# Two layers of a hybrid diffusion backbone on one core: stores taken off SP's queue, and the second layer's modulation vectors made in the first layer's out-projection

## The chip, the cores and the metric

The kernel runs on 1 core of one Trainium2 chip. The metric is the device time of one execution in microseconds. The median of 3 runs of the kernel before is 5156.44 us (5150.59 to 5167.15).

## What is computed

Two layers (DEPTH 2) work on 512 latent tokens and 256 context tokens of width 1024. In the kernel the 768 tokens are six tiles of 128 rows: tiles 0 and 1 are context, 2 to 5 latent. Each layer of the reference, cut to what matters here:

```python
sh_a, sc_a, g_a, sh_f, sc_f, g_f = jnp.split((silu(c) @ w_mod[l] + b_mod[l])[:, None, :], 6, axis=-1)
csh_a, csc_a, cg_a, csh_f, csc_f, cg_f = jnp.split(silu(c_ctx) @ w_mod[l] + b_mod[l], 6, axis=-1)
y_c, y_l = _hybrid_mixer(_modulate(s_ctx, csh_a, csc_a), _modulate(x, sh_a, sc_a), ang, need_ctx,
                         w_in[l], w_out[l], ml, rw, mla)       # mLSTM, RWKV-7, attention; concat @ w_out
x = _ln_affine(ALPHA * x + g_a * y_l, ln_mix_g[l], ln_mix_b[l])
h_l = _modulate(x, sh_f, sc_f)                                 # the context likewise, in the first layer
y = _peer(h, peer_w_q[l], peer_keys[l], peer_u[l], peer_v[l])  # 8 heads, top 16 of 16384 experts
x = _ln_affine(ALPHA * x + g_f * y_l, ln_ffn_g[l], ln_ffn_b[l])
```

The vectors sh, sc and g of a layer depend only on c and c_ctx and on that layer's w_mod (1024 x 6144, 25.2 MB): they can be made at any time before their layer begins.

## The kernel before, in words

**The stages of a layer**, one after the other: modulated input and input projection; attention (`mla`) woven with the mLSTM's projection; the mLSTM woven with RWKV's projection (`mlstm`, `project_rwkv`); `rwkv`; the out-projection (`project_out`) with the residual and LayerNorm of each tile; the PEER ranking (`scores`); then routing and gates, with expert blocks computed early (`early`, 38 of 128 blocks in the first layer, 34 in the second) beside gathers of single experts; the dense stage over all expert blocks (`dense`: A = u·h, gelu and gates, acc += v·c); and the last residual (`final` for gathered tiles, the loop below it for dense ones). In the first layer the dense tiles are the latents 2 to 5 and the gathered ones the context's 0 and 1; in the second 2, 3, 4 and 5.

**Order.** `weave` interleaves generators by the numbers beside them, and a scheduler then fixes one list of instructions for each engine. An engine, and a queue of DMAs that an engine issues, goes through its list in order: an instruction whose inputs or buffers aren't ready holds up what stands behind it. Nearly all loads and stores are issued by SP (`nc.sync`); POOL (`nc.gpsimd`) issues gathers of expert rows (L1601) and a few stores; ACT issues none.

**Modulation** (`modulation`, L320 on). A round r makes 2048 columns: per step k four tiles of 128 x 512 of w_mod (256 KB each, tag "wmod") are loaded (L333) and multiplied with silu(c) into one PSUM bank (L338; g runs 3, 2, 1, 0), eight steps to a round, then bias, transposes, and four stores of the rows to DRAM (L347). The first round of layer 0 stands in the setup. The other two of layer 0 and all three of layer 1 are woven into layer 0's mLSTM stage, with 8 buffers:

```python
gens.append((chain(self.modulation(w, 0, (1, 2), 1, 8), self.modulation(w, 1, (0, 1, 2), 1, 8)), 51))
```

**The out-projection** (L1199 on) loads eight slabs of w_out (tag "wout", 3 buffers), splits each on ACT and DVE into a high and a low part (wo0hi, wo0lo, ...), and for each of the tiles 3, 4, 2, 5, 0, 1 loads the concatenated mixer output (ycat), transposes it and runs 48 matmuls (L1239). The caller runs it to the tenth yield in layer 0, then emits the latents' hidden transposes (`hidden`, L1289), then the rest.

**Early blocks** load ut (L1259), split it (L1266 ACT, L1267 DVE or POOL), run 24 matmuls (L1497), gelu on ACT (tile c, L1499), and store c to DRAM (L1512). Gates are built on PE and ACT in a tile "stage" and stored in four pieces (L1484, 112 of them). Both stores stand on SP's queue between the loads of ut.

**Dense and last residual.** Before the dense stage the residual inputs of the dense tiles (xn, L368), one of the gathered (xr), and a gate row are loaded on SP. Layer 1's modulated input finds the latents kept in SBUF, and loads the context (xt) from DRAM again.

## Time and profile before

| | |
|---|---|
| median of 3 runs | 5156.44 us (5150.59 to 5167.15) |
| the profiled execution's own time | 5153.65 us |
| its span | 5151.7 us |
| mean granted TensorE clock | 0.941 |
| busy: PE, weight loads, DVE, ACT, POOL | 89%, 75%, 71%, 36%, 40% |
| DMA | 991.60 MB, mean 192 GB/s |

The page of the profile has the span in 40 slices: PE is full (9 tenths or more) in two long stretches, the dense stages of the two layers, and at 6 to 9 tenths elsewhere. All times below are microseconds from the start of the span. Layer 0's stages lie about so: mLSTM stage 377 to 628, rwkv to 965, out-projection to 1091 with the start of the ranking, routing and early blocks 1240 to 1645, dense to 2850; layer 1: mLSTM 3222 to 3404, out-projection from 3713, routing and early blocks 3920 to 4189, dense 4199 to 5104. A group of instructions reads "busy, mean ns of one, idle before it and what ended the idle time". In the chain of waits each line is a piece of time and what the end of the span was waiting for in it. A duration of a DMA in the chain runs from its issue to its landing; on a queue ("SPq") it is the time that the queue's issuing took, waits between the issues of one row included.

### The profile page before, as it was taken

How to read it: one execution, taken by the hardware profiler on the slowest of the kernel's cores; microseconds unless marked ns; L12 is line 12 of the kernel's file. 1: busy time of each engine (PE TensorE's matmuls, PEld its weight loads, DVE VectorE, ACT ScalarE, POOL GpSimd, SP SyncE). 2: the span in 40 equal slices, each digit the busy share in tenths (PEclk: the TensorE clock that was granted, in tenths of full speed). 3: DMA queues.
4: the chain of work that ended last, by engine and by line, in shares of the span. 5: the costliest groups of instructions: out<-in, count | busy, mean ns of one | idle time of the engine just before them, and what ended most of it. 6: DMA issues, size and time to landing. Idle time of an engine off the chain costs nothing.

```text
span 5151.7 us, 89696 instructions
## 1 busy us (share of the span) xinstructions
PE 4604.4 (89%) x35473; PEld 3857.8 (75%) x35473; DVE 3676.4 (71%) x7469; ACT 1848.1 (36%) x3330; POOL 2065.0 (40%) x1761
## 2 busy tenths in 40 slices
PE   6998888888987999999999689978778889999998
PEld 4675567667876887778878467767667888988887
DVE  4444455679885999999999734545579757777777
ACT  2342255232553222222222223345433543333332
POOL 1102333244773555555555210233336634444442
PEclk9998889999998999999999898989989999999999
DMA  4016400321477999999999310100222578999994
GB/s 144 22 43 220 159 4 5 122 83 56 170 284 255 352 342 329 347 342 343 346 335 339 104 34 23 45 22 3 85 96 91 214 269 311 320 316 316 315 319 173
DMA packets 402933, 991.60 MB, mean 192 GB/s; under 512 B 35104, under 2 KB 167584, under 8 KB 401744
## 3 DMA queue, kind: packets, MB, share of 16 engines
q1 hardware_dynamic: 289552, 574.91, 32.2%
q0 software_dynamic: 112960, 410.96, 22.1%
q8 instruction: 279, 4.57, 0.4%
q14 instruction: 142, 1.16, 0.1%
HBM read 894.45 MB, written 91.19 MB: 191 GB/s over the span
## 4 chain that ended last, share of the span: by engine, by line
PE 64%; DVE 15%; POOL 6%; DMA 5%; issue 5%; ACT 4%; SPq 1%; POOLq 0%; DVEq 0%; ACTq 0%
PE acc L1564 17%; PE A L1497 15%; PE b L446 6%; PE b L1355 4%; PE spill L1564 3%; PE b L1497 2%; PE b L1239 2%; DMA c<-early 1%; PE b L799 1%; PE b L1479 1%; PE b L826 1%; PE b L530 1%; DVE py L1617 1%; POOL eq L1430 1%; DMA ut<-in_u_t 1%
## 5 line engine op out<-in xcount | busy, mean ns | idle before, releaser
L1601 POOL DMA_INDIRECT rows<-in_u,eid x384 | 538.3, 1402 | 565.6 <-DVE act L1613 251.8
L1601 POOL DMA_INDIRECT rows<-in_v,eid x384 | 517.0, 1346 | 559.2 <-DVE py L1617 324.4
L1564 PE MATMUL acc<-vhi,clo 128*128 128x512 f32 x1536 | 600.8, 391 | 0.0
L1564 PE MATMUL acc<-vt,chi 128*128 128x512 f32 x1536 | 600.5, 391 | 0.0
L1564 PE MATMUL acc<-vhi,chi 128*128 128x512 f32 x1536 | 599.1, 390 | 0.0
L1497 PE MATMUL A<-hh,uhi 128*128 128x384 f32 (+1 forms) x1472 | 541.1, 368 | 25.5 <-ACT uhi L1266 22.7
L1497 PE MATMUL A<-hh,ut 128*128 128x384 f32 (+1 forms) x1472 | 540.1, 367 | 12.5 <-DVE ut L1267 12.5
L1497 PE MATMUL A<-hl,uhi 128*128 128x384 f32 (+1 forms) x1472 | 540.4, 367 | 0.0
L1266 ACT ACTIVATE uhi<-ut 128x1024 fp32r<-128x1024 f32 x256 | 271.1, 1059 | 629.7 <-PE A L1497 521.7
L1617 DVE SCALAR_TENSOR_TENSOR py<-rows,act,py 128x1024 f32<-128x1024 f32 x381 | 492.4, 1292 | 1.9
L1613 DVE CUSTOM_DVE_ANT_0 rows<-rows,hrow 128x1024 f32<-128x1024 f32 x384 | 463.7, 1240 | 12.2 <-DMA rows<-in_u,eid 12.2
L1266 ACT ACTIVATE vhi<-vt 128x1024 fp32r<-128x1024 f32 x256 | 270.8, 1058 | 555.0 <-PE spill L1564 334.6
L446 PE MATMUL b<-hT,winhi 128*128 128x512 f32 (+1 forms) x1360 | 382.3, 372 | 6.7 <-ACT winhi L1266 4.8
L1267 DVE TENSOR_TENSOR ut<-ut,uhi 128x1024 fp32r<-128x1024 f32 x212 | 275.5, 1299 | 119.6 <-ACT uhi L1266 77.7
L1564 PEld LDWEIGHTS acc<-vhi,clo 128*128 128x128 f32 x1536 | 288.8, 188 | 61.2 <-DVE clo L1253 0.3
L1564 PEld LDWEIGHTS acc<-vhi,chi 128*128 128x128 f32 x1536 | 289.0, 188 | 59.0 <-ACT chi L1252 0.3
L1564 PEld LDWEIGHTS acc<-vt,chi 128*128 128x128 f32 x1536 | 289.0, 188 | 58.9
L1497 PEld LDWEIGHTS A<-hh,uhi 128*128 128x128 f32 x1472 | 278.3, 189 | 62.9 <-ACT uhi L1266 23.5
L1497 PEld LDWEIGHTS A<-hh,ut 128*128 128x128 f32 x1472 | 278.6, 189 | 47.1 <-DVE ut L1267 14.1
L1267 DVE TENSOR_TENSOR vt<-vt,vhi 128x1024 fp32r<-128x1024 f32 x256 | 312.2, 1220 | 1.5 <-PE spill L1564 0.6
L1497 PEld LDWEIGHTS A<-hl,uhi 128*128 128x128 f32 x1472 | 278.5, 189 | 36.1
L446 PEld LDWEIGHTS b<-hT,winhi 128*128 128x128 f32 x1360 | 245.9, 204 | 64.7 <-issue 26.1
(544 smaller groups left out, 10560.7 us busy)
## 6 DMA issues: line engine op xcount, KB each, us to landing
ut<-in_u_t SPq DMA_DIRECT2D x256, 512.0 KB
vt<-in_v SPq DMA_DIRECT2D x256, 512.0 KB
gates<-stage SPq DMA_DIRECT2D x112, 512.0 KB
wmod<-in_w_mod SPq DMA_DIRECT2D x160, 256.0 KB
gt<-gates SPq DMA_DIRECT2D x32, 1024.0 KB
win<-in_w_in SPq DMA_DIRECT2D x52, 512.0 KB
gt<-gates SPq DMA_DIRECT2D x32, 768.0 KB
wq<-in_w_q SPq DMA_DIRECT2D x32, 512.0 KB
```

The costliest lines, as they stand in the source:

```text
L446: self.nc.tensor.matmul(ps[:, :n], lhsT=w[u][:, k, :], rhs=self.hT[v][:, k, c:c + n], start=k + u + v == 0, stop=k == KT - 1 and u == 1)
L530: nc.tensor.matmul(pss[t // 2 * 2][:, t % 2 * 256:t % 2 * 256 + 256], lhsT=self.hT[u][:, j * 4 + k, t * 128:(t + 1) * 128], rhs=wi[v][:, k ...
L799: nc.tensor.matmul(ps[:, :w], lhsT=qTs[h][:, t * 128:(t + 1) * 128], rhs=self.kT[:, h, c0:c0 + w], start=True, stop=True)
L1239: nc.tensor.matmul(ps, lhsT=yT[u][:, k, :], rhs=ws[k][v][:, cs], start=k + u + v == 0, stop=k == KT - 1 and u == 1)
L1266: self.nc.scalar.activation(out=hi, in_=x, func=AF.Copy)
L1267: lo_eng.tensor_tensor(out=lo, in0=x, in1=hi.bitcast(F32), op=ALU.subtract)
L1355: nc.tensor.matmul(ps[:, :n], lhsT=(wh, wl)[x][:, k, :], rhs=(hi, lo)[y][:, k, :], start=k + x + y == 0, stop=k == KT - 1 and x == 1)
L1497: nc.tensor.matmul(bank[:, :n], lhsT=us[x][:, k, :], rhs=(hi, lo)[y][:, k, :], start=k + x + y == 0, stop=k == KT - 1 and x == 1)
L1564: nc.tensor.matmul(b, lhsT=cs[x][:, t * 128:(t + 1) * 128], rhs=vs[y][:, h * 512:(h + 1) * 512], start=s0 and x + y == 0, stop=s1 and x == 1)
L1601: nc.gpsimd.indirect_dma_start(out=r, out_offset=None, in_=a[tab], in_offset=bass.IndirectOffsetOnAxis(ap=eid[:, i:i + 1], axis=0))
L1613: nc.vector.tensor_tensor_reduce(out=r, in0=r, in1=h, scale=1.0, scalar=0.0, op0=ALU.mult, op1=ALU.add, accum_out=act[:, i:i + 1])
L1617: nc.vector.scalar_tensor_tensor(out=y, in0=r, scalar=act[:, i:i + 1], in1=y, op0=ALU.mult, op1=ALU.add)
```

## The change

1. **Stores off SP.** The stores of modulation rows (L347), of mLSTM output y (L738), of the mixer residual (L1194, L1651) and the loads of ycat (L1207), and around the last residual the gate row, xn, xr and the vectors, are issued by POOL. The stores of gi and gf (L471, L472), of the attention output (L829), of the gates (L1484) and of the early blocks (L1512) are issued by ACT.
2. **Layer 1's modulation** leaves the mLSTM stage (its number in the weave goes from 51 to 21) and is emitted in layer 0's out-projection, three yields after each of the ten yields of it, with 7 buffers for "wmod".
3. **Room for that:** two buffers for "wout" (3 before), one gate tile for both streams, 6 buffers for gathered rows (`ROWS`, 7 before).
4. **The context's residual tiles stay in SBUF** beside the latents' (xs for all six tiles), so that layer 1 loads no xt; layer 0 loads no xr, and its last residual runs on DVE alone.

```diff
-ROWS = 7
+ROWS = 6
 def modulation(...)
-                nc.sync.dma_start(out=dr[:, r, g], in_=rows[32 * g:32 * g + 2, :])
+                nc.gpsimd.dma_start(out=dr[:, r, g], in_=rows[32 * g:32 * g + 2, :])
...
-            nc.sync.dma_start(out=o[n][0:4, :], in_=msc[r:r + 4, :])
+            nc.scalar.dma_start(out=o[n][0:4, :], in_=msc[r:r + 4, :])
...
-                nc.sync.dma_start(out=self.y[t * 128:(t + 1) * 128, 0:256], in_=yL[:, t, :])
+                nc.gpsimd.dma_start(out=self.y[t * 128:(t + 1) * 128, 0:256], in_=yL[:, t, :])
...
-                nc.sync.dma_start(out=self.y[t * 128:(t + 1) * 128, 640:1024], in_=yM[:, t, :])
+                nc.scalar.dma_start(out=self.y[t * 128:(t + 1) * 128, 640:1024], in_=yM[:, t, :])
...
-                            gens.append((chain(self.modulation(w, 0, (1, 2), 1, 8), self.modulation(w, 1, (0, 1, 2), 1, 8)), 51))
+                            gens.append((self.modulation(w, 0, (1, 2), 1, 8), 21))
...
 def residual(...)
-                (q or nc.sync).dma_start(out=d, in_=x)
+                nc.gpsimd.dma_start(out=d, in_=x)
...
 def project_out(...)
-            nc.sync.dma_start(out=y, in_=self.y[t * 128:(t + 1) * 128, :])
+            nc.gpsimd.dma_start(out=y, in_=self.y[t * 128:(t + 1) * 128, :])
...
-            w = self.t(pw, [128, D], "wout", 3)
+            w = self.t(pw, [128, D], "wout", 2)
...
-            gate = self.gate_rows(p, l, 2, s, f"gate{s}")
+            gate = self.gate_rows(p, l, 2, s, "gate")
...
-                    nc.sync.dma_start(out=G[tk // 32, :, i:i + 32, :], in_=st[:, i:i + 32, :])
+                    nc.scalar.dma_start(out=G[tk // 32, :, i:i + 32, :], in_=st[:, i:i + 32, :])
...
-            self.nc.sync.dma_start(out=done[i], in_=c)
+            self.nc.scalar.dma_start(out=done[i], in_=c)
...
                 out = self.project_out(w, v, l, need, x, hold)
+
+                late = self.modulation(w, 1, (0, 1, 2), 1, 7) if need else iter(())
                 for _ in range(10 if need else 8):
                     next(out)
+                    for _ in range(3):
+                        next(late, None)
                 spans = [self.hidden(pe, w, l, 1, dn if need else dn + ga, [] if need else ga)]
                 hi, lo = (z[:, :, :T * 128] for z in spans[0])
+                self.all(late)
                 self.all(out)
...
-                        nc.sync.dma_start(out=d, in_=x)
+                        nc.gpsimd.dma_start(out=d, in_=x)
...
-                gate = self.gate_rows(ln, l, 5, 1, "gate1")
+                gate = self.gate_rows(ln, l, 5, 1, "gate1", q=nc.gpsimd)
                 xn = self.keep.enter_context(pool("xn", "right")) if need else ln
-                xs = {t: self.load_x(xn, t, f"xn{t}", 1) for t in dn}
+                xs = {t: self.load_x(xn, t, f"xn{t}", 1, nc.gpsimd) for t in dn + (ga if need else [])}
...
-                    xr = {ga[0]: self.load_x(ln, ga[0], "xr", 1)}
...
-                        x = xr[t] if t in xr else self.load_x(ln, t, "xr", 1)
+                        x = xs[t] if need else self.load_x(ln, t, "xr", 1, nc.gpsimd)
...
-                        self.residual(w, l, "f", tiles, [xs[t] for t in tiles], zs, rows, nc.vector if tiles[-1] == TURN[T][-1] else nc.gpsimd, None, FQ and nc.gpsimd, FM and nc.gpsimd)
+                        self.residual(w, l, "f", tiles, [xs[t] for t in tiles], zs, rows, nc.vector if need or tiles[-1] == TURN[T][-1] else nc.gpsimd, None, FM and nc.gpsimd)
```

Where instructions move, the lists of the engines show it. First SP's list where layer 0's out-projection begins, before (gate rows, slabs of w_out, residual inputs xk):

```order
L1207 DMA ycat_10941<-y_149 128x1024
L361 DMA gate_2085_11347<-mod_rows_69 128x1024
L1214 DMA wout_10885<-in_w_out 128x1024
L1214 DMA wout_10891<-in_w_out 128x1024
L1214 DMA wout_10897<-in_w_out 128x1024
L368 DMA xk_2021_10939<-in_x 128x1024
L1214 DMA wout_10903<-in_w_out 128x1024
L1214 DMA wout_10909<-in_w_out 128x1024
L1214 DMA wout_10915<-in_w_out 128x1024
```

and the same place of the changed kernel, where the tiles of w_mod stand among the slabs (96 of them before the keys and w_q of the ranking are loaded):

```order
L332 DMA wmod_10685<-in_w_mod 128x512
L332 DMA wmod_10687<-in_w_mod 128x512
L1212 DMA wout_10541<-in_w_out 128x1024
L1212 DMA wout_10547<-in_w_out 128x1024
L367 DMA xk_1916_10597<-in_x 128x1024
L332 DMA wmod_10689<-in_w_mod 128x512
L367 DMA xk_1958_10774<-in_x 128x1024
L1212 DMA wout_10553<-in_w_out 128x1024
L1212 DMA wout_10559<-in_w_out 128x1024
L332 DMA wmod_10691<-in_w_mod 128x512
```

The seven tiles wmod_10673 to wmod_10689 fill the seven buffers; wmod_10691 is the eighth, and takes the buffer of wmod_10673. On PE of the changed kernel the second step of the modulation stands among the matmuls of the out-projection so:

```order
L1238 MATMUL b_10618<-wo3hi_10561,yT_1918_10601 128x512
L1238 MATMUL b_10644<-wo2hi_10555,yT_1919_10602 128x512
L1238 MATMUL b_10644<-wo3hi_10561,yT_1918_10601 128x512
L337 MATMUL b_10670<-wmod_10691,cvec_75 32x512
L337 MATMUL b_10670<-wmod_10689,cvec_75 32x512
L337 MATMUL b_10670<-wmod_10687,cvec_75 32x512
L337 MATMUL b_10670<-wmod_10685,cvec_75 32x512
L1238 MATMUL b_10795<-wo0hi_10543,yT_1961_10779 128x512
```

Each step begins with the tile that was loaded last, and the step before it ended with wmod_10673. All 24 steps stand ahead of the latents' hidden transposes, the last four of them with nothing between. Then SP's list where layer 0 goes from the early blocks to the dense stage, before:

```order
L1512 DMA early_119_16956<-c_16954 128x512
L1512 DMA early_122_16994<-c_16992 128x512
L1512 DMA early_126_17026<-c_17024 128x512
L368 DMA xn_3167_17045<-x_m_11243 128x1024
L368 DMA xn_3168_17047<-x_m_11039 128x1024
L368 DMA xn_3169_17049<-x_m_11141 128x1024
L368 DMA xn_3170_17051<-x_m_11345 128x1024
L1259 DMA ut_17071<-in_u_t 128x1024
L1259 DMA vt_17073<-in_v 128x1024
L1536 DMA gt_17075<-gates_10870 128x16x128
```

and changed:

```order
L1258 DMA ut_16882<-in_u_t 128x1024
L1258 DMA ut_16923<-in_u_t 128x1024
L1258 DMA ut_16961<-in_u_t 128x1024
L1258 DMA ut_17073<-in_u_t 128x1024
L1258 DMA vt_17075<-in_v 128x1024
L1535 DMA gt_17077<-gates_10528 128x16x128
L1258 DMA vt_17079<-in_v 128x1024
```

The stores of the last early blocks and the loads of xn no longer stand ahead of the dense stage's first ut (ut_17073 here, ut_17071 before).

## Rows read from the trace of the kernel before

**Rows 1.** The page, part 1: busy time, share of the span, instructions.

```profile
PE 4604.4 (89%) x35473; PEld 3857.8 (75%) x35473; DVE 3676.4 (71%) x7469; ACT 1848.1 (36%) x3330; POOL 2065.0 (40%) x1761
```

**Rows 2.** Windows: length, PE PEld DVE ACT POOL busy, granted clock, DMA share, GB/s.

```profile
377.00:628.00 251.00, 221.83 (x1479) 151.35 (x1477) 109.05 (x319) 60.56 (x138) 69.67 (x95) 0.90 0.61 199
...
1240.00:1645.00 405.00, 340.68 (x1949) 298.51 (x1948) 325.42 (x499) 194.09 (x393) 265.02 (x185) 0.92 0.60 218
...
2260.00:2290.00 30.00, 27.64 (x120) 21.92 (x119) 27.26 (x35) 8.16 (x11) 14.26 (x12) 1.00 1.04 396
...
3222.00:3404.00 182.00, 161.02 (x1079) 134.69 (x1077) 92.59 (x232) 58.93 (x131) 59.73 (x81) 0.92 0.12 35
...
3920.00:4189.00 269.00, 232.34 (x1525) 228.67 (x1523) 196.59 (x275) 144.64 (x293) 171.40 (x115) 0.92 0.53 193
```

**Rows 3.** Waits of SP's queue: total us, times, longest.

```profile
SPq L1207 <- DMA y<-yR: 586.1, 2, 306.8
...
SPq L1512 <- ACT c L1499: 266.5, 59, 16.8
```

**Rows 4.** Groups of instructions, PE, 376 to 640: busy, mean ns, idle before.

```profile
L338 PE MATMUL b<-wmod,cvec 128*32 128x512 f32 x320 | 46.1, 650 | 7.6 <-DMA wmod<-in_w_mod 7.5
```

**Rows 5.** Chain of waits, 376 to 640: shares, then start and us.

```profile
by line: PE b L446 32.0%; PE b L338 11.7%; DMA wmod<-in_w_mod 8.3%; PE b L686 4.3%; PE b L653 3.9%; POOL mv L557 3.1%; issue 2.8%; POOL mixed_r L557 2.0%; PE b L672 1.8%; PE b L569 1.7%; PE b L679 1.5%; PE b L701 1.3%; PE b L661 1.2%; POOL 
...
387.63 2.80 DMA wmod<-in_w_mod
...
408.04 4.96 DMA wmod<-in_w_mod
```

**Rows 6.** Timeline of PE, 395 to 425: start, us, what.

```profile
398.09 1.07 PE L338 MATMUL b<-wmod,cvec 128*32 128x512 f32 x8
...
405.63 1.06 PE L338 MATMUL b<-wmod,cvec 128*32 128x512 f32 x8
```

**Rows 7.** Timeline of PE, layer 0's out-projection.

```profile
965.25 0.79 PE L1239 MATMUL b<-wo0lo,yT 128*128 128x512 f32 x1 [1.53 <-DVE wo0lo L1253]
...
1027.70 2.04 PE L1289 MATMUL b<-consts_g,xk 128*128 128x128 f32 x16
```

**Rows 8.** Timeline of SP's queue, layer 1's out-projection.

```profile
3718.44 2.60 SPq L1214 DMA_DIRECT2D wout<-in_w_out  x3
...
3725.26 2.06 SPq L1214 DMA_DIRECT2D wout<-in_w_out  x2
```

**Rows 9.** Timeline of SP's queue, layer 0, from early blocks to dense.

```profile
1609.68 16.20 SPq L1512 DMA_DIRECT2D early<-c  x3
...
1629.95 6.55 SPq L1259 DMA_DIRECT2D vt<-in_v  x1
...
1637.03 0.43 SPq L1259 DMA_DIRECT2D ut<-in_u_t  x1
```

**Rows 10.** Groups of instructions, PE, 1595 to 1665.

```profile
L1497 PE MATMUL A<-hh,uhi 128*128 128x512 f32 x17 | 7.9, 466 | 13.1 <-ACT uhi L1266 11.7 <-ACT c L1499 1.4
...
L1497 PE MATMUL A<-hh,ut 128*128 128x512 f32 x16 | 7.2, 450 | 7.1 <-DVE ut L1267 7.1
```

**Rows 11.** Groups of instructions, PE, 4180 to 4225 (layer 1).

```profile
L1497 PE MATMUL A<-hh,uhi 128*128 128x384 f32 x21 | 8.6, 411 | 12.4 <-ACT uhi L1266 11.0 <-ACT c L1499 1.4
...
L1497 PE MATMUL A<-hh,ut 128*128 128x384 f32 x20 | 8.1, 404 | 5.4 <-DVE ut L1267 5.4
```

**Rows 12.** Timeline of DVE, between the layers; the bracket is its wait.

```profile
2916.52 1.29 DVE L283 BATCH_NORM_STATS2 mdst<-xt 128x6 f32<-128x512 f32 x2 [6.74 <-DMA xt<-x_f]
```

**Rows 13.** Chain of waits, 1240 to 1600.

```profile
1518.34 8.81 DMA ut<-in_u_t
...
1531.77 7.59 DMA ut<-in_u_t
```

**Rows 14.** Timeline of POOL, 2240 to 2260.

```profile
2251.65 0.60 POOL L1194 DMA_DIRECT2D x_f<-xr  x1
```

**Rows 15.** The page, part 5: busy, mean ns, idle before and its end.

```profile
L1613 DVE CUSTOM_DVE_ANT_0 rows<-rows,hrow 128x1024 f32<-128x1024 f32 x384 | 463.7, 1240 | 12.2 <-DMA rows<-in_u,eid 12.2
```

More of the change, by code (lines that the diff above doesn't have):

```diff
@@ L352, in modulation, with gate_rows, rows @@
             yield
-    def gate_rows(self, pool, l, i, s, tag):
+    def gate_rows(self, pool, l, i, s, tag, bufs=1, q=None):
         src = self.mrow[l].rearrange("s r g n -> s (r g n)")[s, i * D:(i + 1) * D]
-        return self.rows(pool, src, D, tag)
-    def rows(self, pool, src, n, tag, bufs=1):
+        return self.rows(pool, src, D, tag, bufs, q)
+    def rows(self, pool, src, n, tag, bufs=1, q=None):
         g = self.t(pool, [128, n], tag, bufs)
-        self.nc.sync.dma_start(out=g, in_=src.partition_broadcast(128))
+        (q or self.nc.sync).dma_start(out=g, in_=src.partition_broadcast(128))
         return g
@@ L1176, in setup, with residual @@
                 pass
-    def residual(self, p, l, which, tiles, xs, zs, rows, eng, hold=None, q=None, mul=None):
+    def residual(self, p, l, which, tiles, xs, zs, rows, eng, hold=None, mul=None):
         nc = self.nc
@@ L1206, in load @@
             y = self.t(p, [128, D], "ycat", 2)
-            nc.sync.dma_start(out=y, in_=self.y[t * 128:(t + 1) * 128, :])
+            nc.gpsimd.dma_start(out=y, in_=self.y[t * 128:(t + 1) * 128, :])
             return y
-        ahead = [load()]
         ws = []
         for k in range(KT):
-            w = self.t(pw, [128, D], "wout", 3)
+            w = self.t(pw, [128, D], "wout", 2)
             nc.sync.dma_start(out=w, in_=a["w_out"][l, :, k])
@@ L1216, in project_out @@
         rows = {"g": self.rows(p, a["lnp"][l, 0], D, "lng"), "b": self.rows(p, a["lnp"][l, 1], D, "lnb")}
+        ahead = [load()]
         for s, tiles in streams:
-            gate = self.gate_rows(p, l, 2, s, f"gate{s}")
+            gate = self.gate_rows(p, l, 2, s, "gate")
             for t in tiles:
```

11 lines of the change are left out of this document (5 added, 6 removed).

## The prediction

> **What bounds the kernel now.** I read the page's shares first: PE is busy 89% of the span, DVE 71%, ACT 36%, POOL 40% [rows 1]. Two dense stages hold some 2,100 us with PE full; the change leaves their work alone, so everything is decided in the stretches where PE has gaps. I then cut the span into windows [rows 2]. Layer 0's mLSTM stage, which carries five rounds of modulation, takes 251 us with 29 us of PE gaps; layer 1's, which carries none, takes 182. Routing with early blocks takes 405 us (PE 341, DVE 325 busy) and 269 us (PE 232). Next came the waits of SP's queue, and here a large number means little: 586 us before L1207 are waits for a mixer output while nothing behind it was due. The 266 us on early blocks' stores waiting for ACT's c (59 times) are different, since loads of ut stand behind them [rows 3]. Last, the chain and the timelines of single places showed which of these waits PE or DVE felt.
>
> **The sum**, against the profiled execution's 5153.65 us, 2.8 below the median of 5156.44.
>
> *a. The mLSTM stage loses three of its five rounds.* Five rounds keep PE busy for 46.1 us, so three are 27.7 [rows 4]. In the chain of that stretch of 264 us the matmuls hold 11.7% (30.9 us) and the waits for wmod 8.3% (21.9 us) [rows 5]; three fifths of both are 31.7. At least the matmuls' share should go (-18). At most, the whole difference between the layers, 69 us, is modulation, and three fifths of it is 41; but layer 1's stage also writes fewer mLSTM outputs. I take -32 (-18 to -41).
>
> *b. Layer 0's out-projection gains them.* That is 24 steps of four tiles, all on PE's list before the latents' hidden transposes. If PE's work were all, 27.7 us would come on top, partly in gaps. But with seven buffers the steps form a chain: a step begins with the tile whose buffer the step before gave up last, as front's lists show. So one step costs four matmuls, 1.07 us [rows 6], and then the whole way of one tile from issue to landing. The chain shows that way at 2.80 us and at 4.96 [rows 5], with up to eight tiles under way in both; here it is four and a slab or two, so I take 3.3, nearer the first. A step is then 4.4 us (3.9 to 6.1); with eight buffers two steps took 405.63 - 398.09 = 7.5 us, 3.8 each [rows 6]. The first step comes 12 matmuls after wo0lo at 965.25, at 968; the last ends at 968 + 23 x 4.4 + 1.1 = 1070, where before the hidden transposes began at 1027.70 [rows 7]. The out-projection's own 62 us fit between the steps. So +43, with the lower end 968 + 23 x 3.9 + 1.1 - 1027.7 = +31 and the upper (6.1) +82. Nothing behind it gives this back: transposes, tile 1 and the ranking follow on PE in the same order, and the loads of keys and w_q stand behind the last wmod on SP.
>
> *c. Two buffers for slabs in layer 1.* Eight slabs go in four turns instead of three; a turn took 3725.26 - 3718.44 = 6.8 us [rows 8], and a turn of two is shorter. +4 (0 to +7). In layer 0 this hides behind the steps of b.
>
> *d. From early blocks to the dense stage.* In layer 0 three stores of early blocks held SP for 16.2 us, then the residual inputs and a vt (6.55), so that a ut was issued only at 1637.03 [rows 9]. PE's first dense matmuls waited 13.1 + 7.1 us for its halves [rows 10]; in layer 1 it was 12.4 + 5.4 [rows 11]. The stores go to ACT, right behind the gelu they wait for, and the xn loads to POOL. Not all 20 and 18 us can go, because the bytes of ut, vt, gates and xn still have to land. I take -14 and -6 (together -5 to -35).
>
> *e. Between the layers.* DVE waited 6.74 us for the reloaded context tile [rows 12]; that load goes, but two additions move to DVE, about 1.2 us each by the row's neighbours of 128 x 1024. -5 (-2 to -12, as PE's own wait there is longer). At the context's last residual PE lost only 2.4 us in 30 [rows 2]; -2.
>
> *f. The early stretch.* Two late ut loads stand in layer 0's chain, 8.81 and 7.59 us [rows 13]; they stood behind gates and early stores. But ACT now issues 184 stores in order with its own work. DVE and POOL bound most of this stretch, so I take -6 (-16 to +16: as much lost if ACT is held up as late loads cost now).
>
> *g. Priced at nothing.* POOL issues some hundred DMAs more; one took 0.60 us [rows 14], 60 us in all, beside some 140 idle in the first early window alone [rows 2]. The smaller ring for gathered rows (six) shortens how far gathers run ahead. DVE waited only 12.2 us for them in the whole span [rows 15]; if the busier POOL and the smaller ring doubled that, it would be +12. The stores of the mLSTM and attention stages stood before loads that weren't due.
>
> Sum: -32 + 43 + 4 - 20 - 7 - 6 = -18, so 5153.65 - 18 = 5135.6, or **5136 us**, 0.4% below the median.
>
> A rule that speaks against the change: in d, rows 9 show a queue standing for 16.2 us in three stores, where one issue on POOL takes 0.60 [rows 14], so what I expect to win is waiting in order, not issue time. The Trainium skill's page "DMA: Bandwidth & Descriptors", in "Issuing engines are not separate DMA queues", says that DMAs of all issuing engines end on the same 16 DMA engines and that issuing from several saves only the time of initiating them. Taken strictly, d and f would be worth almost nothing; the sum by the rule is the third rival's. The row speaks against so strict a reading, as the time at L1512 is a wait for gelu's result and not an issue.
>
> **The rivals.**
>
> *Waits in order were dearer than their chain says (faster).* The gaps of PE in the early stretches are 64 and 37 us [rows 2]; SP's 266 us of waits lie in them [rows 3]. If late loads cause a fifth of that (-20 in place of -6), and d gives -30 in place of -20, the time is 5136 - 24 = 5112. For it: DVE, too, has 80 us of gaps there. Against: only 16.4 us of late ut are in layer 0's chain [rows 13].
>
> *The wmod chain is slower (slower than before).* Place: layer 0's out-projection; price: a step at the upper end, with a landing of 4.96 [rows 5] because slabs of w_out, residual inputs and stores land at the same time, and bias loads on SP that wait for POOL's stores of the round before. A step of 6.1 us makes b +82 and the time 5136 + 39 = 5175. It makes the kernel measurably slower from about 6.0 us a step (36 us more in b than I take). Against: 4.4 us per step is 1 MB in 4.4 us, 238 GB/s, and the chip moved 396 in one window [rows 2].
>
> *Stores on another queue win nothing (no change, or slower).* If the first ut and vt of the dense stage are limited by bytes anyway, as in that section of the skill, then d and f are 0: 5136 + 26 = 5162, inside the bound of no change; with b also a little above its middle (4.9 a step, +11) 5173. Against: the rows of d [rows 9, 10].
>
> *ACT takes the wait over (no change).* ACT's list now holds 184 stores, each behind a wait for its own result or for an earlier DMA; a uhi behind it comes late, and PE with it. f turns to +16 and d loses half: 5136 + 22 + 10 = 5168. For it: PE already waits mainly for uhi [rows 10, 11]. Against: ACT was busy only 194 of 405 us and 145 of 269 [rows 2].
>
> That the modulation moves is certain from the lists, so a change that does nothing isn't among the cases.
>
> **How the numbers follow.** The forecast has 0.46, the dearer waits 0.19, the slower chain 0.14, worthless queues 0.09, ACT's waits 0.12. A measurement of this kernel tells some 0.3% from no change, 15.5 us around 5156: 5141 to 5172. The forecast, 5136, lies close to its lower edge; with b alone between 4.1 and 4.9 us a step it spans 5129 to 5147, and I give 0.34 of it to faster, 0.11 to the same, 0.01 to slower. The dearer waits go to faster (0.19). The slower chain is slower (0.13, and 0.01 the same); worthless queues share out 0.05 same and 0.04 slower; ACT's waits 0.07 same and 0.05 slower. Together: faster 0.53, same 0.24, slower 0.23. The range runs from the dearer waits (5112) with a at -41 and b at +31, which is 21 less: 5091, so 5090, to the slower chain with c at its upper end, 5178, so 5180; beyond lie combinations such as the slower chain with ACT's waits.
>
> **What would show it.** Right: the mLSTM stage of layer 0 near 219 us; in the out-projection a step of wmod every 4 to 5 us with PE waiting on its first tile, and the hidden transposes some 43 us later after wo0lo than the 62 us of before; SP's queue without waits on c and stage; the first dense ut issued with no store before it, and PE's waits there down by half; no wait for xt between the layers. Wrong: steps every 6 us or every 3; ACT's queue with waits of tens of us at its stores; gathers that DVE waits for; or a mLSTM stage that stays above 235 us, which would mean that its chain runs through the mLSTM itself and the modulation was filler.

## The result and the profile after

The change makes the kernel slower: 5197.07 us median of 4 runs (5188.59 to 5198.64) against 5156.7 (5150.59 to 5167.15) for the kernel before on the same chip. The ratio is 1.0079, 95% interval 1.0065 to 1.0092, some 40 us. The profiled execution, the fastest of the four, took 5188.59 us and spans 5186.8 (before 5151.7), so the two traces differ by 35.1 us.

The page, parts 1 and 3 (DMA queues), of the kernel after, to be read beside [rows 1]:

```profile
PE 4603.2 (89%) x35473; PEld 3848.9 (74%) x35473; DVE 3692.7 (71%) x7471; ACT 1850.3 (36%) x3328; POOL 2105.7 (41%) x1831
...
q10 hardware_dynamic: 28000, 77.44, 4.0%
```

The engines do the same work within 0.4%, POOL 2% more; q10 is ACT's DMA queue, which is new. So the 35 us are gaps. These are the windows of layer 0's mLSTM stage and out-projection, and of both early stretches, in the kernel after (length, busy time of PE, PEld, DVE, ACT and POOL, granted clock, DMA share, GB/s):

```profile
372.00:576.00 204.00, 183.63 (x1307) 141.85 (x1305) 106.91 (x301) 60.10 (x137) 75.22 (x106) 0.97 0.36 115
918.00:1049.00 131.00, 99.86 (x475) 55.79 (x476) 68.25 (x199) 22.75 (x25) 14.88 (x21) 0.88 0.79 265
1254.00:1640.00 386.00, 325.46 (x1863) 283.71 (x1862) 327.21 (x502) 189.64 (x383) 263.05 (x183) 0.92 0.55 195
3945.00:4213.00 268.00, 228.54 (x1519) 225.43 (x1518) 206.68 (x339) 142.40 (x293) 168.99 (x113) 0.94 0.52 183
```

Beside [rows 2] the mLSTM stage has lost 47 us of length and a third of its PE gaps, the out-projection has 31 us of gaps, and layer 0's early stretch has 61 us of them. (The early window of [rows 2] reaches 47 us into the stage behind it, so its 64 us of gaps can't be compared with these 61.) Cut at the same matmuls, the early stretch reads so, first before, then after:

```profile
1239.50:1597.80 358.30, 315.59 (x1854) 279.45 (x1853) 321.70 (x499) 185.43 (x382) 256.90 (x180) 0.94 0.57 207
```

```profile
1254.40:1638.80 384.40, 323.86 (x1853) 282.28 (x1853) 326.56 (x499) 188.74 (x381) 262.11 (x182) 0.92 0.55 194
```

PE's gaps there grew by 17.8 us, from 42.7 to 60.5; the other 8.3 us are longer busy time at a lower granted clock.

To compare kernels I cut every span at the same matmuls, by their first or last start. The last three columns apart, all are layer 0's: *mLSTM* runs from attention's last matmul of queries with keys to RWKV's last projection, *to hidden* from there to the latents' first hidden transpose (RWKV and out-projection, where the moved rounds lie), *early* from the last ranking matmul to the last gates matmul, *transition* from there to the first accumulating matmul of the dense stage, *dense* to its last one. *Trans. 1* is the transition of layer 1, *end* runs from the last dense matmul to the end of the span. All in us:

| kernel | mLSTM | to hidden | early | transition | dense | trans. 1 | end | span |
|---|---|---|---|---|---|---|---|---|
| before | 257.5 | 402.8 | 358.3 | 61.4 | 1226.1 | 42.7 | 23.6 | 5151.7 |
| after | 203.8 | 473.8 | 384.4 | 49.6 | 1236.5 | 37.6 | 27.9 | 5186.8 |
| mod_only | 204.5 | 485.7 | 359.3 | 61.0 | 1229.6 | 42.9 | 23.7 | 5183.4 |
| stores_only | 241.5 | 412.7 | 382.6 | 50.1 | 1235.3 | 37.3 | 27.9 | 5168.6 |
| early_gates_on_sp | 209.3 | 476.6 | 359.6 | 60.4 | 1232.8 | 40.3 | 27.9 | 5180.7 |
| gates_on_sp | 206.5 | 483.4 | 357.8 | 47.9 | 1232.9 | 38.2 | 28.0 | 5167.0 |
| early_on_sp | 207.9 | 476.3 | 377.1 | 59.0 | 1231.8 | 41.5 | 27.9 | 5190.6 |
| split_first | 208.6 | 474.1 | 371.3 | 49.4 | 1232.8 | 37.2 | 28.0 | 5164.2 |
| gates_one_store | 211.9 | 479.4 | 379.5 | 53.4 | 1241.1 | 37.7 | 27.9 | 5202.1 |
| split_one | 203.7 | 473.2 | 369.6 | 47.8 | 1238.9 | 38.2 | 27.9 | 5159.7 |
| g_order | 210.2 | 477.5 | 382.4 | 50.0 | 1230.4 | 38.6 | 27.9 | 5190.5 |
| slabs3_w5 | 210.2 | 507.8 | 384.2 | 50.6 | 1236.4 | 37.4 | 27.9 | 5224.8 |
| rest_only | 243.6 | 405.3 | 357.8 | 60.3 | 1231.9 | 40.1 | 28.0 | 5140.5 |
| best1 | 241.9 | 404.1 | 359.7 | 53.6 | 1233.3 | 37.7 | 28.0 | 5130.5 |
| best2 | 239.9 | 404.4 | 362.2 | 44.6 | 1239.5 | 37.2 | 25.1 | 5125.8 |
| best3 | 239.9 | 405.3 | 392.5 | 37.5 | 1238.0 | 35.7 | 25.6 | 5162.7 |

Each row is one execution. The nine kernels that have the mLSTM stage of the kernel after unchanged take 203.7 to 211.9 us there, with granted clocks from 0.97 down to 0.92, so a few us in one cell mean little.

The 35.1 us of after are made up of these differences: +4.3 before the mLSTM stage, -53.7 in it, +71.0 to the hidden transposes, -6.7 to the last ranking matmul, +26.1 early, -11.8 transition, +10.4 dense, -9.0 from the last dense matmul to layer 1's modulating transposes, then in layer 1 +5.9 in the out-projection, -0.6 in what lies around it and in its early stretch, -5.1 transition, and +4.3 at the end.

### The profile page after: what moved, and what is told of

It reads as the page before. It is cut to its first block, busy times and chain, and to the rows that moved or that the text cites. A ratio compares the mean times of both kernels' runs of the same rounds, so it can differ in the third digit from the quotient of the medians.

```text
span 5186.8 us, 89551 instructions
## 1 busy us (share of the span) xinstructions
PE 4603.2 (89%) x35473; PEld 3848.9 (74%) x35473; DVE 3692.7 (71%) x7471; ACT 1850.3 (36%) x3328; POOL 2105.7 (41%) x1831
## 4 chain that ended last, share of the span: by engine, by line
PE 62%; DVE 16%; POOL 8%; DMA 6%; issue 5%; ACT 4%; ACTq 0%; SPq 0%; POOLq 0%; DVEq 0%
PE acc L1563 17%; PE A L1496 15%; PE b L445 5%; PE b L1354 4%; PE spill L1563 3%; PE b L1496 2%; DMA c<-early 2%; PE b L1478 2%; DMA wmod<-in_w_mod 1%; PE b L798 1%; POOL eq L1429 1%; DVE py L1616 1%; PE b L529 1%; PE b L825 1%; PE b L337 1%
## 5 line engine op out<-in xcount | busy, mean ns | idle before, releaser
L1496 PE MATMUL A<-hh,ut 128*128 128x384 f32 (+1 forms) x1472 | 541.3, 368 | 11.8 <-DVE ut L1266 11.8
L1612 DVE CUSTOM_DVE_ANT_0 rows<-rows,hrow 128x1024 f32<-128x1024 f32 x384 | 468.9, 1253 | 13.2 <-DMA rows<-in_u,eid 13.1
L445 PE MATMUL b<-hT,winhi 128*128 128x512 f32 (+1 forms) x1360 | 371.0, 363 | 2.7 <-POOL hT L388 2.4
L1496 PE MATMUL b<-hh,ut 128*128 128x512 f32 (+1 forms) x576 | 221.1, 384 | 66.5 <-POOL ut L1266 49.2
## 6 DMA issues: line engine op xcount, KB each, us to landing
gt<-gates SPq DMA_DIRECT2D x32, 1024.0 KB, 13.2
```

Of the source, the lines that this page charges most:

```text
L445: self.nc.tensor.matmul(ps[:, :n], lhsT=w[u][:, k, :], rhs=self.hT[v][:, k, c:c + n], start=k + u + v == 0, stop=k == KT - 1 and u == 1)
L1496: nc.tensor.matmul(bank[:, :n], lhsT=us[x][:, k, :], rhs=(hi, lo)[y][:, k, :], start=k + x + y == 0, stop=k == KT - 1 and x == 1)
L1612: nc.vector.tensor_tensor_reduce(out=r, in0=r, in1=h, scale=1.0, scalar=0.0, op0=ALU.mult, op1=ALU.add, accum_out=act[:, i:i + 1])
```

## The experiments

Two questions were put: whether the move of the modulation or the stores lose the time, and by which mechanism. Edits are against the kernel after unless said otherwise.

**mod_only**: the kernel before with the move alone (also the two slab buffers, the single gate tile and the six row buffers that it needs); all stores and loads stay on their old queues.

```diff
-    gens.append((chain(self.modulation(w, 0, (1, 2), 1, 8), self.modulation(w, 1, (0, 1, 2), 1, 8)), 51))
+    gens.append((self.modulation(w, 0, (1, 2), 1, 8), 21))
...
+    late = self.modulation(w, 1, (0, 1, 2), 1, 7) if need else iter(())
```

> The kernel before with layer 1's modulation moved as in the change and with its price in room (two slab buffers, one gate tile, six gather buffers), all stores where they were before. Theory A: the early stretch is as before (356 to 364), and what is left is the move itself: the mLSTM stage shorter by 45 to 55, the out-projection with rwkv's end longer by 60 to 72, layer 1's out-projection longer by 4 to 7; sum +10 to +25, time 5167 to 5182. Theory B with the gather ring as cause: the early stretch 375 to 390 here too, time 5185 to 5200.

5184.14 us, ratio 1.0061 (1.0039 to 1.0084). The move alone loses 28 us: -53.0 in the mLSTM stage, +82.9 to the hidden transposes, more than the 60 to 72 that were expected, which puts the time 2 us above its range. The early stretch is as before (359.3), so neither the move nor the smaller ring of gather buffers costs it anything.

**stores_only**: the other half, everything but the move.

```diff
-    late = self.modulation(w, 1, (0, 1, 2), 1, 7) if need else iter(())
+    late = iter(())
```

(and the chain of five rounds back in the mLSTM's weave)

> The changed kernel with layer 1's modulation back in layer 0's mLSTM stage; all stores, the room made (two slab buffers, six gather buffers) and the kept context tiles as in the change. Theory A: the early stretch stays at 380 to 388, the mLSTM stage comes back to 245 to 258, the out-projection to 65 to 75 from its first matmul; time 5175 to 5190. If moving the modulation is what costs the early stretch (another start state of gathers and loads), it falls to 358 to 365 and the time to 5150 to 5165.

5169.11, ratio 1.0026 (1.0016 to 1.0036). The stores, too, lose on balance. They win 16.0 in the mLSTM stage and 11.3 at the transition, and lose 9.9 before the hidden transposes (where slabs have two buffers), 24.3 in the early stretch and 4.3 at the end. So both halves are losses, each in another place. The time is 6 us under the expected range; the early stretch was as expected.

**early_gates_on_sp**: the stores of early blocks and of gates back on SP.

```diff
-    nc.scalar.dma_start(out=G[tk // 32, :, i:i + 32, :], in_=st[:, i:i + 32, :])
+    nc.sync.dma_start(out=G[tk // 32, :, i:i + 32, :], in_=st[:, i:i + 32, :])
...
-    self.nc.scalar.dma_start(out=done[i], in_=c)
+    self.nc.sync.dma_start(out=done[i], in_=c)
```

> The changed kernel with the stores of the gates and of the early blocks back on SP's queue, nothing else. In the changed kernel layer 0's early stretch (last ranking matmul to last gates matmul) takes 384.7 us against 358.6 before, and the way from there to the first dense accumulation 50.3 against 62.1. Theory A, the two kinds of stores on ACT cost the early stretch its 26 us (through ACT's order or ACT's waits): the stretch falls back to 356 to 364, the transition grows back to 58 to 64, and the time falls by 8 to 22 us, to some 5175 to 5189. Theory B, the stretch grew for another reason (POOL's added stores, the smaller gather ring, the later start): the stretch stays at 380 to 390, the transition grows by some 10, and the time is 5197 to 5212.

5184.26, ratio 1.0061 (1.0038 to 1.0083). The early stretch is back at 359.6, but the transition's gain is gone too (60.4): two stores, one of them good and one bad.

**gates_on_sp** and **early_on_sp** take them apart: only the first or only the second of those two lines goes back to SP.

> The changed kernel with only the gates' stores (112, in groups of four) back on SP; the early blocks' stores (72) stay on ACT. ACT's list has the split two blocks ahead for about half of the blocks. A1 (order): the early stretch falls about half way, 366 to 376. A2 with the groups of four as the holding: it falls nearly all the way, 358 to 366. If the early stores behind the gelu are what holds ACT: 378 to 386. The transition, which is decided by the early stores, stays at 47 to 53.

> The changed kernel with only the early blocks' stores back on SP; the gates' stores stay on ACT. ACT's list has the split one block ahead for nearly all blocks. A1 (order): the early stretch stays at 376 to 386. A2 with the early stores as the holding: 358 to 368. The transition grows back to 57 to 63, since its three late stores stand on SP again.

gates_on_sp 5167.68, ratio 1.0025 (1.0013 to 1.0038); early_on_sp 5201.11, ratio 1.0094 (1.0077 to 1.0111). With the gates' stores on SP the early stretch takes 357.8 and the transition keeps its 47.9; the other way round it is 377.1 and 59.0. The gates' stores on ACT cost 17 to 27 us there; the early blocks' stores on ACT cost nothing by themselves, and 7 where the gates' stores are on ACT too. For the theory of the order, gates_on_sp is a miss: that theory expected 366 to 376, and the stretch fell all the way, as the theory of ACT being held by the groups of four had it. What ACT and PE waited for in layer 0's early stretch (us in total, times, longest), first in the kernel after, then before, then gates_on_sp:

```profile
ACT c L1498 <- PE b L1496: 79.8, 20, 14.7
...
PE b L1496 <- POOL ut L1266: 20.1, 4, 8.3
...
PE b L1496 <- DVE ut L1266: 15.6, 7, 6.9
...
ACT oh L1458 <- DMA gates<-stage: 5.8, 2, 3.2
```

```profile
ACT c L1499 <- PE b L1497: 23.5, 5, 12.8
...
PE b L1497 <- POOL ut L1267: 10.9, 2, 8.8
```

```profile
ACT c L1498 <- PE b L1496: 42.4, 12, 15.2
...
PE b L1496 <- POOL ut L1266: 11.8, 3, 8.8
...
PE b L1496 <- DVE ut L1266: 0.4, 1, 0.4
```

ACT hardly waits for its stores (5.8 us). What has grown is its wait at the gelu c for PE, and PE's wait for the split of the next block (ut), from 10.9 to 35.7 us. The rows of ACT's timeline show how; after, then before:

```profile
1350.12 1.06 ACT L1265 ACTIVATE uhi<-ut 128x1024 fp32r<-128x1024 f32 x1
1350.26 2.88 ACTq L1483 DMA_DIRECT2D gates<-stage  x4
1353.50 0.60 ACT L1498 ACTIVATE c<-b 128x512 f32<-128x512 f32 x1 [2.32 <-PE b L1496]
...
1361.41 1.06 ACT L1265 ACTIVATE uhi<-ut 128x1024 fp32r<-128x1024 f32 x1
1364.32 0.60 ACT L1498 ACTIVATE c<-b 128x512 f32<-128x512 f32 x1 [1.85 <-PE b L1496]
```

```profile
1326.45 1.06 ACT L1266 ACTIVATE uhi<-ut 128x1024 fp32r<-128x1024 f32 x1 [4.68 <-PE b L1497]
1327.42 0.58 ACT L1499 ACTIVATE c<-b 128x512 f32<-128x512 f32 x1
...
1335.81 1.06 ACT L1266 ACTIVATE uhi<-ut 128x1024 fp32r<-128x1024 f32 x1 [1.35 <-issue]
1336.77 0.58 ACT L1499 ACTIVATE c<-b 128x512 f32<-128x512 f32 x1
```

Before, ACT splits a block (uhi) when PE has just finished another, and the gelu of the finished one follows without a wait: in ACT's list 21 of layer 0's 38 early gelus have the splits of two later blocks ahead of them. After, it is 3 of 38: ACT takes up the gelu of a block that PE is still computing, stands there, and the next split comes later. In gates_on_sp it is 15. So the stores changed the scheduled order of ACT's whole list; the count alone doesn't follow the time, since 15 are enough for 357.8.

**gates_one_store** puts a rival to that, the time that ACT spends issuing: one store for four.

```diff
-    for i in range(0, 128, 32):
-        nc.scalar.dma_start(out=G[tk // 32, :, i:i + 32, :], in_=st[:, i:i + 32, :])
+    nc.scalar.dma_start(out=G[tk // 32], in_=st)
```

> The changed kernel with the gates' stores still on ACT, but each group of four stores of 512 KB made one store of 2 MB; ACT's list has the split one block ahead of the gelu everywhere, as in the changed kernel. If ACT is held by issuing the groups (2.9 us each on its queue, 28 groups in layer 0, 81 us), the early stretch falls from 384 to 362 to 374, the half that emitting the split first did not give back, and the time by 8 to 20, to 5177 to 5189. If all of it is the order on ACT's list, of which emitting the split first mended only a part, the stretch stays at 379 to 387 and the time at 5192 to 5200.

5192.25, ratio 1.0071 (1.0055 to 1.0087); its profiled execution was the slowest of its four. A group of issues shrinks from 2.88 us to 0.33, some 41 us for layer 0's 16 groups (the 28 of the expectation are those of both layers), but the early stretch only from 384.4 to 379.5. Issue time is at most a small part of the cause; the order (again 3 of 38) is unchanged.

**split_first** leaves all queues as they are and writes the early blocks in another order: two blocks kept loaded and split, and the split after next emitted between a block's matmuls and its gelu.

```diff
-    nxt = self.load_u(p, l, blocks[0], eng(0))
+    nxt = [self.load_u(p, l, blocks[n], eng(n)) for n in range(2)]
...
+    if n + 2 < len(blocks):
+        nxt.append(self.load_u(p, l, blocks[n + 2], eng(n + 2)))
+    c = self.t(p, [128, w], "c", 3)
+    self.nc.scalar.activation(out=c, in_=bank[:, :w], func=AF.Gelu_apprx_tanh)
```

> The changed kernel, with the stores of the gates and of the early blocks on ACT as in the change; only the early generator is written in another order: the split of the block after next is emitted between a block's matmuls and its gelu. ACT's list then has the split (uhi) two blocks ahead of the gelu for most blocks, as in the kernel before and in the run with those stores back on SP; in the changed kernel it is one block ahead everywhere from the eighth on. Theory A1, the order on ACT's list costs the 25 us: layer 0's early stretch falls from 384 to 356 to 368, and the transition to the dense stage stays at 47 to 53, so the time falls by 15 to 28 to 5168 to 5182. Theory A2, ACT is held up by the stores' own waits and issue: the stretch stays at 378 to 388 and the time at 5190 to 5200.

5166.46, ratio 1.0031 (1.002 to 1.0042), by the ratios some 25 us less than after. The early stretch gets half of its loss back (371.3, between the ranges of the two theories), layer 1's falls from 267.3 to 259.1. 30 of 38 gelus now have two splits ahead of them, more than before. In layer 0's early stretch ACT waits less at the gelu and PE less for splits, but more for POOL's one-hots (the tiles oh that the gates' matmuls take; 19.5 in the kernel after):

```profile
ACT c L1513 <- PE b L1509: 20.4, 4, 11.4
...
PE b L1478 <- POOL oh L1455: 29.8, 8, 7.2
...
PE b L1509 <- POOL ut L1266: 14.2, 3, 8.4
...
PE b L1509 <- DVE ut L1266: 3.4, 2, 3.0
```

**split_one** has both of these edits.

> The changed kernel with both: the split of an early block emitted before the gelu, and each group of four gates' stores on ACT made one store. The order on ACT's list is that of the run with the split alone, where layer 0's early stretch took 371 of the changed kernel's 384 (358 with the gates on SP). If the 13 us that are left come from ACT issuing the groups, the stretch falls to 358 to 366. If they come from the rest of the order on ACT's list, it stays at 368 to 374; the time then is as with the split alone, 5160 to 5172.

5173.8, ratio 1.0047 (1.0029 to 1.0065); early 369.6. Issue time and splits together don't explain the 11 us that stay above before's 358.3. They go with the gates' stores: best1 below has the same order of the program with these stores on SP, and takes 359.7 (its modulation is back in the weave as well, which by mod_only is nothing to this stretch). By which way the stores cost them (PE's longer wait for one-hots is one sign) stays open.

**g_order** turns to the moved modulation: the four tiles of a step are used in the order in which their buffers come free.

```diff
-                    for g in (3, 2, 1, 0):
+                    for g in ((0, 1, 2, 3) if bufs == 7 else (3, 2, 1, 0)):
```

> The changed kernel, with the four tiles of a step of the moved modulation multiplied in the order in which they are loaded (0 to 3) instead of 3 to 0; the result is the same, the same seven buffers. The tile that a step begins with then took its buffer three tiles earlier. If the steps are a chain of one matmul group and one whole landing (4.2 to 4.4 us from step to step in the changed kernel, PE waiting 3.1 to 3.4 for a landing in most), the steps come every 3.2 to 3.8 us here, the hidden transposes of the latents begin 10 to 22 us earlier, and the time is 5175 to 5188. If the DMA engines' rate or PE's list sets the pace, nothing moves by more than 4 us: 5193 to 5200.

5197.41, ratio 1.0089 (1.007 to 1.0107): no gain, in the range that was expected if the DMA engines' rate or PE's list sets the pace. The waits at the moved modulation's matmuls (us, times), first in the kernel after, then here:

```profile
  DMA wmod<-in_w_mod: 59.6, 35
```

```profile
  DMA wmod<-in_w_mod: 16.2, 13
```

The chain through the landings is broken, and the time goes elsewhere: steps now fall apart into single tiles among the out-projection's matmuls, which PE's timeline shows at nearly the price of a whole step.

```profile
960.93 1.04 PE L337 MATMUL b<-wmod,cvec 128*32 128x512 f32 x2
...
974.71 1.05 PE L337 MATMUL b<-wmod,cvec 128*32 128x512 f32 x2
```

One tile takes 1.04 us where a step's four take 1.07 [rows 6]. In the out-projection the modulation's matmuls keep PE busy for twice as long; after, then here:

```profile
L337 PE MATMUL b<-wmod,cvec 128*32 128x512 f32 x192 | 29.0, 680 | 25.4 <-DMA wmod<-in_w_mod 25.4
```

```profile
L337 PE MATMUL b<-wmod,cvec 128*32 128x512 f32 x192 | 57.0, 627 | 4.8 <-DMA wmod<-in_w_mod 4.7
```

**slabs3_w5** gives slabs of w_out their third buffer back and the modulation five in place of seven (a slab has the size of two of its tiles).

```diff
-            w = self.t(pw, [128, D], "wout", 2)
+            w = self.t(pw, [128, D], "wout", 3)
...
-                late = self.modulation(w, 1, (0, 1, 2), 1, 7) if need else iter(())
+                late = self.modulation(w, 1, (0, 1, 2), 1, 5) if need else iter(())
```

> The changed kernel with three buffers for the slabs of w_out again, and five instead of seven for the moved w_mod tiles, which just fits. In the changed kernel the first six steps come every 6 us, beside a chain of slabs that land 5 to 7.5 us after each other's release, and the later 18 every 4.2 to 4.4 us between landings. If slabs hold the first part, the sixth step comes 8 to 14 us sooner after the first matmul (32 us in the changed kernel), and layer 1's out-projection takes 61 to 63 us from its first matmul to the transposes instead of 65.4. With five buffers, three of a step's four tiles are issued only after the step before has ended, so the later steps should take 5.0 to 5.8 us; together the hidden transposes of layer 0 come 2 to 18 us later than in the changed kernel: 5196 to 5212. If the later steps are set by the rate of the DMA engines instead, they stay at 4.2 to 4.6, and the time is 5178 to 5192.

5229.09, ratio 1.0152 (1.0136 to 1.0168). The wait for wmod doubles:

```profile
  DMA wmod<-in_w_mod: 127.6, 38
```

The time is 17 us above the expected range. The first five steps were no faster (29 us from the first to the fifth, for 25), and the later ones came 6.7 us apart on average (5.0 in the kernel after), so buffers of the steps are worth more here than a slab's.

**rest_only** is the change without its three costly parts: modulation back in the weave, three slab buffers, and both stores of the early stretch on SP.

> What is left of the change without the modulation's move and without the gates' and early blocks' stores on ACT: the other stores off SP, the context tiles kept, six gather buffers, three slab buffers as before. From the milestones: the mLSTM stage 10 to 15 us shorter than before (242 of 257), the out-projection as before, the early stretch 356 to 362, the transition 58 to 62, layer 1's out-projection as before (58 to 61 from its first matmul to the transposes). Sum -8 to -18 against the kernel before: 5138 to 5148. If the 14 us of the mLSTM stage are lost again in the stages behind, as half of them were in the run with all stores: 5150 to 5158.

5147.25, ratio 0.9989 (0.9978 to 1.0): the rest (stores of the mixers, residuals and loads on POOL and ACT, residual inputs kept) is worth some 6 us (0 to 11): 14 in the mLSTM stage, as expected, while the end takes 4.4 more.

**best1** is rest_only with the early stores on ACT and split_first's order. **best2** goes on: no DMA at all on ACT (early stores on POOL, the mixers' on SP). **best3** is best2 with the gates' stores on POOL.

```diff
-    self.nc.scalar.dma_start(out=done[i], in_=c)
+    self.nc.gpsimd.dma_start(out=done[i], in_=c)
```

> The parts of the change that the runs so far price as gains: modulation in the mLSTM stage and three slab buffers as before, gates' stores on SP, early blocks' stores on ACT, all other stores off SP, context tiles kept; with the split of an early block emitted before the gelu. From the milestones: mLSTM stage -14, transition to dense -12 in layer 0 and -3 to -5 in layer 1, early stretch of layer 1 -5 to -8 by the split, layer 0's early stretch 350 to 360 (0 to -8), end of the span +4. Sum -28 to -40 against the kernel before: 5114 to 5127. If early stores on ACT with the gates on SP cost layer 0's early stretch 10 us or more in this surrounding: 5130 to 5140.

> The same, but no store at all on ACT: gi, gf and the attention output on SP as before, the early blocks' stores on POOL. All kernels with a DMA on ACT so far end 27.9 us after the last dense matmul, those without (before, and the modulation alone) 23.6. If ACT's queue being in use costs that, the end is at 23 to 24 here and 4 us are won against the version with early stores on ACT: 5110 to 5123. If POOL, waiting in order for the gelu, delays its own halves and gathers, the early stretch of layer 0 grows to 365 or more and the time is 5125 to 5145, with the end at 23 to 24 all the same.

> The fastest version so far (no store on ACT, early blocks' stores on POOL) with the gates' stores on POOL too, so that SP issues no store in the early stretch. If what costs is only that ACT's list changes, nothing is lost (layer 0's early stretch 355 to 364) and the transition may gain another 2 us: 5122 to 5132. If gates' stores cost on any engine that works in this stretch, POOL's halves come late and the stretch grows by 8 us or more: 5136 to 5155.

best1 5132.54, ratio 0.996 (0.9947 to 0.9973). best2 5127.98, ratio 0.995 (0.9938 to 0.9962): it beats both kernels, by some 25 us the one before. best3 5163.81, ratio 1.0023 (1.0013 to 1.0033). The times of best1 and best2 lie some 5 us above the better of their two ranges, and best3's 9 us above the worse. So the gates' stores cost 30 us in the early stretch on POOL as well (392.5 for 362.2), where PE waits for the one-hots that POOL makes (34.7 us in best2); in best3:

```profile
PE b L1478 <- POOL oh L1455: 42.2, 13, 11.2
```

On POOL the issues alone take 34.6 us of its time, so there issue time is not excluded as the cause. The gates' stores cost on both working engines that were tried; on SP, which has nothing else to do, they cost nothing that shows (357.8 to 362.2, before 358.3).

## Why the prediction was wrong

I forecast 5136 us; it is 5197, outside the range and on the other side of before. The steps, against the profiled executions:

*a, the mLSTM stage (-32, at most -41): -53.7.* Right in sign, and beyond its bound. mod_only alone gives -53.0. The stage between the same two matmuls, before and in mod_only ([rows 2] begins 10 us later):

```profile
367.40:624.90 257.50, 229.32 (x1512) 158.02 (x1510) 111.08 (x325) 60.33 (x136) 67.66 (x94) 0.89 0.59 193
```

```profile
368.30:572.80 204.50, 187.76 (x1308) 145.25 (x1306) 106.07 (x301) 59.71 (x136) 67.83 (x93) 0.94 0.35 115
```

PE is busy 41.6 us less, where three rounds' matmuls are 27.7; the rest of this saving goes with a granted clock of 0.94 (0.97 after) in place of 0.89, for which I had no term. The other 11.4 us are gaps, close to the 13 that I took for the waits. Stores_only shows 16.0 us for the stores alone in the same stage, and these don't add to the move's: after has -53.7 with both.

*b, the out-projection (+43, at most +82): +71.0,* and +82.9 in mod_only. The chain of steps was right, what lies between and ahead of the steps was not. This is the kernel after's chain of waits from 905 to 1090 (shares; then start and us):

```profile
by line: DMA wmod<-in_w_mod 29.2%; PE b L1238 15.7%; PE b L337 14.0%; DMA wout<-in_w_out 10.1%; DMA ycat<-y 4.4%; DVE hh L1291 2.7%; issue 2.4%; DVE md1w L271 1.6%; ACT hm L1290 1.5%; POOL hl L1292 1.4%; DVE mdst L282 1.3%; PE b L1227 1.1%;
...
906.34 8.06 DMA ycat<-y
...
921.64 7.45 DMA wout<-in_w_out
...
932.67 5.16 DMA wout<-in_w_out
...
940.21 6.05 DMA wout<-in_w_out
...
954.12 1.08 PE b L337 x8
955.20 3.32 DMA wmod<-in_w_mod
958.57 1.08 PE b L337 x8
...
974.71 10.66 PE b L1238 x46
```

An undisturbed step from 954 on is 1.08 and a landing of 3.32, 4.4 us, just as I had it. But the steps came 5.2 us apart on average, and two sentences failed. "The out-projection's own 62 us fit between the steps": behind the last slab 18 us of its matmuls stand on the chain, 10.66 of them in one piece. And "In layer 0 this hides behind the steps of b": three landings of slabs stand on the chain, 18.7 us, and the first five steps came 6.2 us apart. Of the 28 us over my term some 10 lie ahead of the out-projection's first matmul, where ycat's 8.06 us stand on the chain; some 3 (7, less 4 by which the first step came earlier than I had it) in the steps beside the slabs; 12 between the later steps; and 3 behind the last one. POOL issues ycat in the kernel after, and its first load also stands behind the slabs in the program, an edit that the list of the change doesn't show. It takes both halves of the change: mod_only and stores_only have 1 us each there. What stood first on SP's queue there, from its timeline:

```profile
840.14 65.47 SPq L332 DMA_DIRECT2D wmod<-in_w_mod  x6
905.72 0.85 SPq L1212 DMA_DIRECT2D wout<-in_w_out  x2
```

The first slabs are issued only at 905.72, behind six wmod loads whose issuing, waits included, holds SP for 65 us. That hold isn't what the loss needs: in mod_only the first slabs go out at 886.74, 19 us ahead of the first matmul that uses them, and the loss is larger. No run takes the parts of the 28 us apart; with one more slab buffer and two fewer for the steps (slabs3_w5) the start was no better. The rival of the slower chain came nearest in time (5175), but by steps of 6.1 us and landings of 4.96, which are not what happened. Together a and b come to +17.3 where I had +11: two errors of over 20 us that nearly cancel, which is luck.

*f, the early stretch (-6, at most +16): +26.1. This is the step that failed.* I wrote "ACT now issues 184 stores in order with its own work" and bounded its harm by what late loads cost now. The gates' stores on ACT cost 17 to 27 us there (gates_on_sp, early_on_sp, early_gates_on_sp). Half of it is the order of splits and gelus on ACT's list: split_first gives 13 back. Waits at the stores (5.8 us) and issue time (5 us of 26 by gates_one_store, 2 by split_one) are small parts; how the gates' stores cost the other 11 to 13 stays open. Of the rivals, the one in which ACT takes the wait over pointed to the right engine and to a late uhi, but it put the lateness down to waits at the stores and, at +16, priced it too low. It also counted the lost half of the transition, which did not happen. "ACT was busy only 194 of 405 us" was no argument: an engine half idle still lost the others' time when its list took things up in another order. The late loads that were to go had been worth little: with the early stores off SP, gates_on_sp takes 357.8 where before took 358.3.

*d, the transitions (-14 and -6): -11.8 and -5.1.* Right, at the place that I named. PE's groups at the first dense matmuls of layer 0, after:

```profile
L1496 PE MATMUL A<-hh,uhi 128*128 128x512 f32 x24 | 12.0, 498 | 7.7 <-ACT c L1498 5.5 <-ACT uhi L1265 2.3
L1496 PE MATMUL A<-hh,ut 128*128 128x512 f32 x24 | 11.8, 490 | 1.6 <-DVE ut L1266 1.6
```

The idle time fell from 20.2 us [rows 10] to 9.3. So the strict reading of the Trainium skill's page "DMA: Bandwidth & Descriptors", section "Issuing engines are not separate DMA queues", by which another issuing engine saves only issue time, does not hold here: early_on_sp has a transition of 59.0 and after 49.6, and what was saved is waiting in order. But in layer 0 the dense stage grew by 10.4 us. Its windows, before and after:

```profile
1659.20:2885.30 1226.10, 1201.58 (x5185) 973.06 (x5183) 1146.46 (x1500) 349.67 (x446) 650.06 (x487) 1.00 0.92 331
```

```profile
1688.40:2924.90 1236.50, 1208.41 (x5184) 977.61 (x5183) 1149.29 (x1500) 349.60 (x446) 654.80 (x494) 0.99 0.92 329
```

Only 3.6 of the 10.4 us are gaps of PE; 6.8 are longer busy time, with a granted clock of 0.99 for 1.00. DVE's waits for the reload of early blocks grew from 19.0 us to 26.5 within the stage. Whether the gain of the transition is given back here is not shown: the five kernels with a transition of 59 us or more take 1226.1 to 1232.8 in the dense stage, the others 1230.4 to 1241.1, and the ranges overlap.

*e and c.* Between the layers -9.0 for -7, and no wait for xt is left; c was +5.9 for +4. *g* held: gathers cost no more than 1 us in DVE's waits, from 12.2 [rows 15] to 13.2.

*Not foreseen*: +4.3 before the mLSTM stage, not traced, and +4.3 at the end.

So the sum failed by +32 in f, +28 in b, +10 in dense and +9 in the two places not foreseen, against -22 in a, -7 between the hidden transposes and the last ranking matmul (where I had written that nothing gives b back) and +2 in smaller terms; the median lies another 8.5 us above the profiled execution.

## What to carry to other kernels

Here, of two kinds of stores that wait for their data, one won by leaving the queue of an engine with nothing else to do (the early blocks', at the transition) and one lost (the gates'). So show on the chain what a store delays before it is moved, and where it is moved to a working engine, read that engine's whole new list (which instruction it now stands at, and what stood ahead of it before), not its busy share. Where work is moved out of a stage, price what the new place has to share at its start (here buffers and the first loads) and the work that stands between its steps as carefully as the steady step. A change in two parts that both lose can hold parts that win: without the move, with the gates' stores back on SP, the early blocks' stores off it and the split written ahead of the gelu (best2), this kernel gains 25 us.

## What the runs showed of the hardware

The end of the span goes with whether ACT has issued DMAs. The last store's issue, after and before:

```profile
5176.85 0.54 POOL L1193 DMA_DIRECT2D out<-xn  x1 [1.79 <-DVE xn L1187]
```

```profile
5146.04 0.53 POOL L1194 DMA_DIRECT2D out<-xn  x1 [1.80 <-DVE xn L1188]
```

From there to the end of the span it is 10.0 us after and 5.7 before. In all kernels of the table with an end of 27.9 or 28.0, ACT issues DMAs; in those without, the end takes 23.6 to 25.6. What makes the difference was not traced; in best2, where 23 to 24 were expected without ACT's DMAs, it is 25.1, so they are not all of it. Also unexpected: one tile of modulation alone takes PE 1.04 us where four in a row take 1.07 (g_order).
